# One stream of the dilated attention works in the recurrence's inverse tiles

## The chip, the core and the metric

One core of one Trainium2 chip runs the whole block. The metric is the device time of one execution in microseconds (us); lower is better. The engines are TensorE (PE in the profile, PEld its weight loads), VectorE (DVE), ScalarE (ACT), GpSimd (POOL) and SyncE (SP), which issues the DMAs in its own program order.

## What is computed

A decoder block over 1024 tokens of width 1024, in float32: a normalised and modulated input goes through one projection; mixer A is a gated delta rule with 8 heads, mixer B a dilated window attention with three groups of four heads; both are gated, projected, merged, projected again and added to the input.

```python
h = rms_norm(x, norm_w) * (1 + scale) + shift
qa, ka, va, za, beta, a, qb, kb, vb, zb, ga, gb = split(h @ w_in)
o_a = gated_delta_rule(l2(silu(conv(qa))), l2(silu(conv(ka))), silu(conv(va)), g(a), sigmoid(beta))
y_a = (rms_norm(o_a) * silu(za)) @ w_proj_a
for window, dilation in ((128, 1), (512, 4), (2048, 16)):   # 4 heads of 64 each
    o_g, lse_g = dilated_window_attention(qb, kb, vb, window, dilation)
y_b = (o_b * softmax_over_groups(lse) * silu(zb)) @ w_proj_b
x = x + gate * ((sigmoid(ga) * y_a + sigmoid(gb) * y_b) @ w_out)
out = rms_norm(x, final_norm_w)
```

In the delta rule, each chunk needs the inverse of a triangular matrix: `t_inv` is applied to the values in every step of the recurrence.

## The kernel before

The program is written by a planner. Each piece of work is a generator (a "stream") with a priority; `Sched.run` keeps an estimated clock for each engine and, whenever TensorE's estimated clock allows, steps the ready stream of the lowest priority number. So the order of every engine's instructions comes out of estimates at build time. On the chip each engine then runs its list in that order and waits by semaphores.

The main stream, `projections` (priority 99), fills TensorE with products of 512 columns: h and each weight are split into a high and a low part of reduced float32, and three products (high-high, high-low, low-high) give the accuracy. It goes over single projections first, then over seven pairs (`pair`, seven products of blocks for a two-by-two block product instead of eight), of which the last, `z8`, makes two of mixer B's gates with a silu in `block_sink`; then come the products of the merges (`tail_products`: `pa_step` for w_pa, two tiles of output interleaved at first, then w_pb) and w_out. In the profile's names pj and sb are PSUM tiles, wr and wh a weight raw and split, big a 128x1024 tile of SBUF, mid a 128x512 one.

The recurrence of mixer A runs beside the projections. `merge_stream` puts the chunk inverses of head h together in `TT[h % 2]`, one of two constant tiles of 128x8x128, and `rec_stream` reads them in its eight steps; when it is through it sets `ev_ttfree[h]`.

The attention is a list `todo_a` of 24 units: 3 groups x 2 pairs of heads x 4 pairs of blocks of 128 tokens. A worker, `attn_work`, takes the next unit, waits until the projections it reads are stored, and runs `attn_unit`: loads of q, k and v into one tile (three DMAs), scores on TensorE into two PSUM tiles, a masked maximum on VectorE into a second tile, the exponential on ScalarE there, transposes on TensorE, their copies on ScalarE, the product over the values on TensorE, a copy on VectorE, and a store to DRAM (ogd). Both tiles come from the pool `big` of 34 tiles: `big.many(2)` waits until two are free, and `big.put()` gives one back. Three workers share the list (`WORKERS = 3`, priorities 6.0 to 6.2), so up to three units are under way.

When all eight units of a group are done, `ev_og[g]` is set, and statistics of the groups are combined. `ya_split` (two streams, priority 8) reads the stored outputs of mixer A (yad), one head after the other, into two `mid` halves and splits them for the merges' products. It begins with `ev_tail`, set when the last pair begins, and takes two big tiles a head; until the last group is done it leaves `RESERVE` = 4 of them.

Of the kernel before, what the change touches and what calls it, by code (L numbers as in the profile page):

```python
# [35 lines left out]
BLOCKS = ("B11", "T2", "T1", "B21", "T3", "B22", "T4")  # L36
BLK = "x3"
BLK1 = "T1 T3 T3 T5"
WORKERS = 3
RESERVE = 4  # L40
HPRIO = 8
NW = 8
# [243 lines left out]
def hybrid_block_kernel(ctx: ExitStack, tc: tile.TileContext, x, c, norm_w, ada_w, ada_b, w_tiles, w_vb0, w_vb1,  # L286
                        w_vb2, conv_w, a_log, dt_bias, dn_norm_w, w_pa, w_pb, w_out, final_norm_w, consts, out):
    nc = tc.nc
    S = Sched(nc)
# [13 lines left out]
    big = Slots(S, bigp, "big", NBIG, [P, T])  # L303
# [7 lines left out]
    def const(shape, name, dtype=F32):  # L311
        return cp.tile(shape, dtype, name=name)
# [23 lines left out]
    TT = [const([P, 8, P], f"TT{i}") for i in range(2)]  # L336
# [901 lines left out]
    ev_ttfree = [Event() for _ in range(H)]  # L1238
# [322 lines left out]
    ev_og = [Event() for _ in range(3)]  # L1561
    pend = [0, 0, 0]

    def attn_unit(g, i2, ti):

        i0 = 2 * i2
        kf = max(i0 - 1, 0) if g == 0 else i0
        n_ = i0 + 2 - kf
        buf, sm2 = yield from big.many(2)
        qt, kt = buf[:, 0:256], buf[:, 256:256 + n_ * P]  # L1570
        v3 = buf[:, 640:640 + n_ * P].rearrange("p (a f) -> p a f", f=P)
        sp.dma_start(qt, qb_d[2 * g + ti][:, i0 * P:(i0 + 2) * P])
        sp.dma_start(kt, kb_d[2 * g + ti][:, kf * P:(i0 + 2) * P])
        if g == 0:
            src = vb_d[g].rearrange("(i p) f -> p i f", p=P)[:, kf:kf + n_]
        elif g == 1:
            src = vb_d[g].rearrange("(b p r) f -> r p b f", b=2, r=4)[i2]
        else:
            src = vb_d[g].rearrange("(p r) f -> p r f", r=8)[:, i0:i0 + 2]
        sp.dma_start(v3, src[:, :, ti * P:(ti + 1) * P])  # L1580
        yield
        tiles = []
        for i in (i0, i0 + 1):
            prev = (g == 0 and i > 0) or (g == 1 and i % 2 == 1)
            tiles.append((i, i % 2, (i - 1 if prev else i) - kf, 256 if prev else 128))
        sms = [sm2[:, sl] for sl in HALVES]
        pbs = yield from sb.many(2)
        for i, a, k0, nk in tiles:
            for hd in range(2):
                r = slice(64 * hd, 64 * hd + 64)  # L1590
                pe.matmul(pbs[hd][:, a * 256:a * 256 + nk], qt[r, a * P:(a + 1) * P], kt[r, k0 * P:k0 * P + nk], start=True,
                          stop=True)
        yield
        for hd in range(2):
            h4 = 2 * ti + hd
            sm = sms[hd]
            for i, a, k0, nk in tiles:
                msk = amask2 if g == 2 else amask if nk == 256 else amask[:, P:2 * P]
                dve.tensor_tensor_reduce(sm[:, a * 256:a * 256 + nk], pbs[hd][:, a * 256:a * 256 + nk], msk, -0.125, 3e38,
                                         op0=OP.add, op1=OP.min, accum_out=st_a[g][:, i, h4, 0:1])  # L1600
            sb.put()
            yield
            for i, a, k0, nk in tiles:
                s_ = sm[:, a * 256:a * 256 + nk]
                act.activation(s_, s_, AF.Exp, bias=st_a[g][:, i, h4, 0:1], scale=-1.0,
                               accum_out=st_a[g][:, i, h4, 1:2])
        yield
        pts = []
        for hd in range(2):
            pb = yield from sb.get()  # L1610
            n = 0
            for i, a, k0, nk in tiles:
                for b in range(nk // P):
                    pe.transpose(pb[:, n * P:(n + 1) * P], sms[hd][:, a * 256 + b * P:a * 256 + (b + 1) * P], ident)
                    n += 1
            yield
            pt = sms[hd]
            act.activation(pt[:, 0:n * P], pb[:, 0:n * P], AF.Copy)
            sb.put()
            pts.append(pt)  # L1620
        yield
        pb = yield from sb.get()
        n = 0
        for i, a, k0, nk in tiles:
            nb = nk // P
            for b in range(nb):
                for hd in range(2):
                    vv = v3[:, k0 + b, hd * 64:hd * 64 + 64]
                    pe.matmul(pb[64 * hd:64 * hd + 64, a * P:(a + 1) * P], vv, pts[hd][:, n * P:(n + 1) * P],
                              start=b == 0, stop=b == nb - 1)  # L1630
                n += 1
        yield
        big.put()
        dve.tensor_copy(pts[0][:, 0:2 * P], pb[:, 0:2 * P])
        sb.put()
        yield
        sp.dma_start(og_d[2 * g + ti][:, 2 * i2 * P:2 * (i2 + 1) * P], pts[0][:, 0:2 * P])
        big.put()
        pend[g] += 1
        if pend[g] == 8:  # L1640
            S.set(ev_og[g])

    def attn_work():
        while todo_a:
            g, ti, i = todo_a.pop(0)
            yield [ev_vbd[g], ev_qb[2 * g + ti], ev_kb[2 * g + ti], *ev_hb["T4"]]
            yield from attn_unit(g, i, ti)

    todo_a = [(g, ti, i) for g in range(3) for ti in range(2) for i in range(4)]

# [17 lines left out]
    def combine(g):  # L1668
        yield ev_sg
        scr = yield from mid.get()  # L1670
        sa = scr[:, 0:192].rearrange("p (i n) -> p i n", i=8)
        zt = scr[:, 192:288].rearrange("p (i g h) -> p i g h", i=8, g=3)
        zu = scr[:, 288:320].rearrange("p (i h) -> p i h", i=8)
        fg = fg_a[g]
        fi = fg.rearrange("p h i -> p i h")
        if g == 0:
            sp.dma_start(sa, st_d.rearrange("(i p) g n -> p i (g n)", p=P))
        elif g == 1:
            sv = st_d.rearrange("(b p r) g n -> r p b (g n)", r=4, b=2)
            s4 = sa.rearrange("p (r b) n -> p r b n", b=2)  # L1680
            for r in range(4):
                sp.dma_start(s4[:, r], sv[r])
        else:
            sp.dma_start(sa, st_d.rearrange("(p i) g n -> p i (g n)", p=P))
        yield
        s5 = sa.rearrange("p i (g h s) -> p i g h s", g=3, s=2)
        dve.tensor_tensor(zu, s5[:, :, 0, :, 0], s5[:, :, 1, :, 0], op=OP.min)
        dve.tensor_tensor(zu, zu, s5[:, :, 2, :, 0], op=OP.min)
        for q in range(3):
            dve.tensor_tensor(zt[:, :, q], zu, s5[:, :, q, :, 0], op=OP.subtract)  # L1690
        S.chain("dve", 3)
        yield
        act.activation(zt, zt, AF.Exp)
        yield
        for q in range(3):
            dst = zu if q == 0 else fi
            dve.tensor_tensor(dst, zt[:, :, q], s5[:, :, q, :, 1], op=OP.mult)
            if q:
                dve.tensor_tensor(zu, zu, fi, op=OP.add)
        dve.reciprocal(zu, zu)  # L1700
        dve.tensor_tensor(fi, zt[:, :, g], zu, op=OP.mult)
        S.chain("dve", 7)
        yield
        pb = yield from sb.get()
        pe.transpose(pb[0:32, 0:P], fg.rearrange("p h i -> p (h i)"), ident)
        yield
        act.activation(scr[0:32, 320:320 + P], pb[0:32, 0:P], AF.Copy)
        sb.put()
        yield
        sp.dma_start(fg_d[g], scr[0:32, 320:320 + P])  # L1710
        mid.put()
        yield
        S.set(ev_fg[g])
# [10 lines left out]
    ev_tail = Event()  # L1724
# [12 lines left out]
    ya_todo = list(range(8))  # L1737

    def ya_split():
        yield ev_tail  # L1740
        while ya_todo:
            h = ya_todo.pop(0)
            yield ev_ya[h]
            yield lambda: len(big.free_at) > big.debt + 1 + (0 if ev_og[2].t else RESERVE)
            hi = yield from big.get(F32R)
            lo = yield from big.get(F32R)
            ts = yield from mid.many(2)
            for q in range(2):
                sp.dma_start(ts[q], ya_d[h][:, q * 512:q * 512 + 512])
            yield  # L1750
            for q in range(2):
                act.activation(hi[:, q * 512:q * 512 + 512], ts[q], AF.Copy)
            yield
            for q in range(2):
                sl = slice(q * 512, q * 512 + 512)
                dve.tensor_tensor(lo[:, sl], ts[q], hi[:, sl].bitcast(F32), op=OP.subtract)
            mid.put(2)
            YA[h] = (hi, lo)
            S.set(ev_yas[h])
# [242 lines left out]
        S.add(attn_group(g), 7 + g * 0.01, f"attn{g}")  # L2002
    for g in range(3):
        S.add(combine(g), 7.5, f"combine{g}")
    for q in range(WORKERS):
        S.add(attn_work(), 6 + 0.1 * q, f"attnw{q}")
    S.add(ya_split(), 8, "yas")
    S.add(ya_split(), 8.1, "yas")
    S.add(yb_split(), 8, "ybs")
    S.add(yb_split(), 8, "ybs")  # L2010
# [70 lines left out]
```

## Time and profile before

| | |
|---|---|
| median of 3 runs | 1279.53 us (1276.94 to 1280.24) |
| the profiled execution | 1279.4 us, its span 1277.7 us |
| granted TensorE clock, mean | 0.995 |
| busy: PE, PEld, DVE, ACT, POOL | 98%, 81%, 60%, 39%, 14% |
| DMA | 172.03 MB, mean 135 GB/s |
| ACT table loads in 860 to 1060 us | 5, of 1283 ns |

Times within the span count from its first instruction. All instructions are issued through one helper, so every row has line L129 and is told apart by its tiles. A busy TensorE is the union of pipelined, overlapping products (a 512-wide one lasts about 0.4 us, and the next begins about 0.23 us after it); products in full float32 (scores, values) show as two. The last group of the attention falls between about 985 and 1046 us.

### The profile page before, as it was taken

What the parts mean: (1) busy time and instruction counts of PE and PEld (TensorE: products, weight loads), DVE (VectorE), ACT (ScalarE), POOL (GpSimd) and SP (SyncE); (2) the same over time, 40 slices, a digit from 0 to 9 for tenths busy, and PEclk for the clock granted to TensorE, in tenths of its full rate; (3) what the DMA queues carried; (4) which work ended last, traced back from release to release, by engine and by line L of the source; (5) the groups of instructions that cost most, each with busy time, mean ns of one, the idle gap of its engine ahead of it and who ended that gap; (6) DMA issues with size and microseconds to landing.
All of it is one profiled execution on the core that took longest, in us unless ns stands there. A gap on an engine that the chain in (4) does not pass through costs nothing.

```text
span 1277.7 us, 19213 instructions
## 1 busy us (share of the span) xinstructions
PE 1252.2 (98%) x7302; PEld 1030.8 (81%) x7302; DVE 766.9 (60%) x1528; ACT 497.9 (39%) x1079; POOL 173.9 (14%) x128
## 2 busy tenths in 40 slices
PE   7999999999999999999999999999999999999997
PEld 3689888988888978888888888887777678878886
DVE  5845893457874367864579834555555546655533
ACT  5525622346223345233462335325555852122211
POOL 4700300033001022000320002300000000002400
PEclk9999999999999999999999999999999999999999
DMA  9534433143322262341343222645455758843422
GB/s 356 200 109 148 120 92 88 67 155 114 112 75 75 73 209 65 102 115 69 107 127 103 83 76 78 225 149 156 145 137 149 251 178 255 231 162 113 143 94 83
DMA packets 112558, 172.03 MB, mean 135 GB/s; under 512 B 41009, under 2 KB 72913, under 8 KB 112466
## 3 DMA queue, kind: packets, MB, share of 16 engines
q1 hardware_dynamic: 112322, 170.55, 42.4%
q8 instruction: 57, 0.93, 0.3%
q14 instruction: 35, 0.29, 0.1%
q10 hardware_dynamic: 144, 0.26, 0.1%
HBM read 123.40 MB, written 47.37 MB: 134 GB/s over the span
## 4 chain that ended last, share of the span: by engine, by line
PE 88%; DVE 3%; DMA 3%; ACT 2%; issue 2%; POOL 1%; SPq 0%; POOLq 0%; ACTq 0%; DVEq 0%
PE pj L129 67%; PE sb L129 22%; DVE big L129 2%; ACT big L129 1%; DMA wr<-in_w_out_dram 1%; DMA big<-kbd 1%; POOL big L129 1%; DMA big<-gd 0%; ACT wh L129 0%; DVE mid L129 0%; DVE wh L129 0%; DMA wr<-in_w_pa_dram 0%; POOL wh L129 0%; ACT L129 0%; SPq L129 0%
## 5 line engine op out<-in xcount | busy, mean ns | idle before, releaser
L129 PE MATMUL pj<-big,wh 128*128 128x512 f32 x3356 | 825.2, 398 | 0.8 <-DVE big L129 0.5
L129 PEld LDWEIGHTS pj<-big,wh 128*128 128x128 f32 x3356 | 617.2, 189 | 131.9 <-issue 9.9
L129 ACT ACTIVATE wh<-wr 128x1024 fp32r<-128x1024 f32 (+3 forms) x99 | 97.5, 985 | 239.7 <-PE pj L129 223.1
L129 DVE TENSOR_TENSOR wh<-wr,wh 128x1024 fp32r<-128x1024 f32 (+3 forms) x96 | 115.2, 1200 | 64.2 <-ACT wh L129 64.0
L129 ACT ACTIVATE big<-big 128x1024 f32<-128x1024 f32 (+2 forms) x77 | 74.1, 969 | 187.2 <-DVE big L129 133.3
L129 PE MATMUL pj<-wh,big 128*128 128x256 f32 (+2 forms) x702 | 110.6, 308 | 0.5 <-POOL wh L129 0.3
L129 PE MATMUL sb<-big,wh 128*128 128x512 f32 x368 | 105.1, 423 | 0.0
L129 PEld LDWEIGHTS pj<-wh,big 128*128 128x128 f32 x702 | 96.2, 189 | 6.2 <-POOL wh L129 0.7
L129 DVE SCALAR_TENSOR_TENSOR big<-pj,cw,big 128x1023 f32<-128x1023 f32 (+2 forms) x72 | 92.1, 1279 | 1.7
L129 PEld LDWEIGHTS sb<-big,wh 128*128 128x128 f32 x368 | 66.9, 190 | 21.1 <-issue 8.4
L129 DVE TENSOR_TENSOR big<-big,big 128x1024 f32<-128x1024 f32 (+4 forms) x44 | 57.8, 1316 | 25.9 <-ACT big L129 18.8
L129 PE MATMUL sb<-sq,big 128*128 128x128 f32 x464 | 67.9, 278 | 3.0 <-ACT sq L129 2.2
L129 PEld LDWEIGHTS sb<-sq,big 128*128 128x128 f32 x464 | 63.4, 193 | 8.8 <-ACT sq L129 3.1
L129 POOL TENSOR_TENSOR wh<-wr,wh 128x1024 fp32r<-128x1024 f32 x3 | 9.1, 3036 | 348.8 <-ACT wh L129 348.8
L129 ACT ACTIVATE big<-sb 128x512 f32<-128x512 f32 (+2 forms) x80 | 40.9, 522 | 39.6 <-PE sb L129 39.5
L129 DVE SCALAR_TENSOR_TENSOR sq<-sq,gsm,sb 128x128 f32<-128x128 f32 x48 | 16.6, 345 | 63.4 <-PE sb L129 62.2
L129 DVE CUSTOM_DVE_ANT_0 big<-sb,cst 128x128 f32<-128x128 f32 (+1 forms) x96 | 29.0, 348 | 39.7 <-PE sb L129 39.7
L129 PEld LDWEIGHTS sb<-cst,big 128*128 128x128 f32 x268 | 33.9, 145 | 22.7 <-DVE rstd L129 6.8
L129 PE MATMUL sb<-cst,big 128*128 128x128 f32 x268 | 43.5, 284 | 8.0 <-DVE rstd L129 4.9
L129 PE MATMUL pj<-big,big 128*128 128x512 f32 x210 | 49.2, 390 | 0.0
L129 ACT ACTIVATE mid<-sb 128x512 f32<-128x512 f32 (+3 forms) x48 | 24.0, 500 | 60.9 <-PE sb L129 60.5
L129 DVE TENSOR_TENSOR mid<-big 64x31 f32<-64x31 f32 (+15 forms) x124 | 41.2, 332 | 8.4 <-POOL big L129 4.9
(140 smaller groups left out, 1283.5 us busy)
## 6 DMA issues: line engine op xcount, KB each, us to landing
wr<-in_w_tiles_dram SPq DMA_DIRECT2D x64, 512.0 KB, 4.2
big<-in_ada_w_dram SPq DMA_DIRECT2D x24, 512.0 KB, 9.0
big<-in_x_dram SPq DMA_DIRECT2D x16, 512.0 KB, 5.2
gd<-big SPq DMA_DIRECT2D x16, 512.0 KB, 2.9
big<-gd SPq DMA_DIRECT2D x16, 512.0 KB, 5.2
big<-grow SPq DMA_DIRECT2D x8, 512.0 KB, 5.7
vtd<-big SPq DMA_DIRECT2D x8, 512.0 KB, 2.6
big<-vtd SPq DMA_DIRECT2D x32, 128.0 KB, 4.5
```

Of the source, the lines that this page charges most:

```text
L129: r = f(*a, **k)
```

## The change

One of the three workers gets its two tiles for good: `TT[0]` for q, k and v and `TT[1]` for the scores. It starts when all eight recurrences are done (`ev_ttfree`), has priority 5.9, ahead of the other workers, and neither takes nor returns big tiles; the other two workers are as before. So the attention holds at most four big tiles at a time instead of six. `ya_split` may begin when either the last pair has begun or the last group is done.

```diff
--- before.py
+++ after.py
@@ -36,7 +36,7 @@
 BLOCKS = ("B11", "T2", "T1", "B21", "T3", "B22", "T4")
 BLK = "x3"
 BLK1 = "T1 T3 T3 T5"
-WORKERS = 3
+WORKERS = 2
 RESERVE = 4
 HPRIO = 8
 NW = 8
@@ -1561,12 +1561,12 @@
     ev_og = [Event() for _ in range(3)]
     pend = [0, 0, 0]
 
-    def attn_unit(g, i2, ti):
+    def attn_unit(g, i2, ti, own):
 
         i0 = 2 * i2
         kf = max(i0 - 1, 0) if g == 0 else i0
         n_ = i0 + 2 - kf
-        buf, sm2 = yield from big.many(2)
+        buf, sm2 = own or (yield from big.many(2))
         qt, kt = buf[:, 0:256], buf[:, 256:256 + n_ * P]
         v3 = buf[:, 640:640 + n_ * P].rearrange("p (a f) -> p a f", f=P)
         sp.dma_start(qt, qb_d[2 * g + ti][:, i0 * P:(i0 + 2) * P])
@@ -1630,21 +1630,25 @@
                               start=b == 0, stop=b == nb - 1)
                 n += 1
         yield
-        big.put()
+        if not own:
+            big.put()
         dve.tensor_copy(pts[0][:, 0:2 * P], pb[:, 0:2 * P])
         sb.put()
         yield
         sp.dma_start(og_d[2 * g + ti][:, 2 * i2 * P:2 * (i2 + 1) * P], pts[0][:, 0:2 * P])
-        big.put()
+        if not own:
+            big.put()
         pend[g] += 1
         if pend[g] == 8:
             S.set(ev_og[g])
 
-    def attn_work():
+    def attn_work(own=None):
+        if own:
+            yield ev_ttfree
         while todo_a:
             g, ti, i = todo_a.pop(0)
             yield [ev_vbd[g], ev_qb[2 * g + ti], ev_kb[2 * g + ti], *ev_hb["T4"]]
-            yield from attn_unit(g, i, ti)
+            yield from attn_unit(g, i, ti, own)
 
     todo_a = [(g, ti, i) for g in range(3) for ti in range(2) for i in range(4)]
 
@@ -1737,7 +1741,7 @@
     ya_todo = list(range(8))
 
     def ya_split():
-        yield ev_tail
+        yield lambda: ev_tail.t is not None or ev_og[2].t is not None
         while ya_todo:
             h = ya_todo.pop(0)
             yield ev_ya[h]
@@ -2002,6 +2006,7 @@
         S.add(attn_group(g), 7 + g * 0.01, f"attn{g}")
     for g in range(3):
         S.add(combine(g), 7.5, f"combine{g}")
+    S.add(attn_work([t_.rearrange("p a b -> p (a b)") for t_ in TT]), 5.9, "attnw")
     for q in range(WORKERS):
         S.add(attn_work(), 6 + 0.1 * q, f"attnw{q}")
     S.add(ya_split(), 8, "yas")
```

The order is the same up to the first unit of attention and again from the third output tile of the merges on. Between, the planner places almost every row of the attention anew. Below, big, TT, sb and pj are followed by their numbers; sta is a unit's statistics.

ScalarE, where the silus of the last pair's blocks (mid onto itself) meet the exponentials of the last group. Before:

```order
L129 ACT_TABLE_LOAD
L129 ACTIVATE mid128_8899<-mid128_8899 128x512
L129 ACTIVATE big241_8766<-sb389_8875 128x256
L129 ACTIVATE wh174_8891<-wr75_8805 128x1024
L129 ACTIVATE mid127_8869<-mid127_8869 128x512
L129 ACTIVATE wh176_8959<-wr76_8908 128x1024
L129 ACTIVATE mid122_8782<-mid122_8782 128x512
L129 ACT_TABLE_LOAD
L129 ACTIVATE big247_8856,sta2_105<-big247_8856,sta2_105 128x128 x2
```

After:

```order
L129 ACT_TABLE_LOAD
L129 ACTIVATE mid128_8939<-mid128_8939 128x512
L129 ACTIVATE mid127_8876<-mid127_8876 128x512
L129 ACT_TABLE_LOAD
L129 ACTIVATE TT1_101,sta2_105<-TT1_101,sta2_105 128x128 x2
L129 ACTIVATE big234_8923<-mid129_8944 128x512
L129 ACTIVATE big234_8923<-mid130_8945 128x512
L129 ACTIVATE wh176_8991<-wr76_8901 128x1024
L129 ACT_TABLE_LOAD
L129 ACTIVATE mid124_8809<-mid124_8809 128x512
L129 ACT_TABLE_LOAD
L129 ACTIVATE TT1_101,sta2_105<-TT1_101,sta2_105 128x128 x2
```

All three silus stood between two table loads; now the third comes later, and a set of exponentials (TT1), a merge input (big234) and the split of a weight (wh176) stand between it and the other two, with two more table loads around it.

TensorE, in the last group, beside the first merge products (pj72, pj73 before and after): transposes (cst), products over values (64x128) and products of 512. Before, the 19th and the 20th unit:

```order
L129 MATMUL sb396_9019<-cst_83,big247_8856 128x128 x2
L129 MATMUL sb397_9023<-cst_83,big247_8856 128x128 x2
L129 MATMUL pj72_8966<-big248_8880,wh172_8744 128x512 x2
L129 MATMUL pj72_8966<-big249_8881,wh172_8744 128x512 x2
L129 MATMUL pj72_8966<-big248_8880,wh173_8867 128x512 x2
L129 MATMUL sb398_9038<-big247_8856,big246_8855 64x128 x4
L129 MATMUL sb399_9043<-cst_83,big253_8942 128x128 x2
L129 MATMUL pj73_9049<-big242_8790,wh174_8891 128x512 x2
L129 MATMUL sb400_9053<-cst_83,big253_8942 128x128 x2
L129 MATMUL pj73_9049<-big243_8791,wh174_8891 128x512 x2
```

After, the 20th to the 22nd unit:

```order
L129 MATMUL sb403_9061<-cst_83,TT1_101 128x128 x2
L129 MATMUL sb404_9065<-cst_83,TT1_101 128x128 x2
L129 MATMUL sb405_9073<-cst_83,big239_8951 128x128 x2
L129 MATMUL sb406_9076<-TT1_101,TT0_100 64x128 x4
L129 MATMUL sb407_9088<-cst_83,big239_8951 128x128 x2
L129 MATMUL sb408_9113<-big239_8951,big238_8950 64x128 x4
L129 MATMUL sb409_9118<-cst_83,big241_8967 128x128 x2
L129 MATMUL pj72_8998<-big236_8927,wh172_8771 128x512 x2
L129 MATMUL sb410_9129<-cst_83,big241_8967 128x128 x2
L129 MATMUL pj72_8998<-big237_8928,wh172_8771 128x512 x2
```

Before, one unit's product stood between transposes of the next with merge products between them; now the transposes of three units and the products of two follow each other with one pair of merge products in between.

SyncE, where the own stream's 18th unit is stored and its next, the 20th, loaded; before, a place with the same kind of rows, where the 19th is stored and the 22nd loaded:

```order
L129 DMA ogd4_190<-big247_8856 128x256
L129 DMA big260_9057<-qbd5_179 128x256
L129 DMA big260_9057<-kbd5_185 128x256
L129 DMA big260_9057<-vbd2_119 128x2x128
L129 DMA mid135_9073<-yad5_125 128x512
L129 DMA mid136_9087<-yad5_125 128x512
L129 DMA ogd4_190<-big253_8942 128x256
L129 DMA big264_9102<-qbd5_179 128x256
```

After:

```order
L129 DMA wr76_8901<-in_w_pa_dram 128x1024
L129 DMA ogd4_190<-TT1_101 128x256
L129 DMA TT0_100<-qbd4_178 128x256
L129 DMA TT0_100<-kbd4_184 128x256
L129 DMA TT0_100<-vbd2_119 128x2x128
L129 DMA mid129_8944<-yad2_122 128x512
L129 DMA mid130_8945<-yad2_122 128x512
L129 DMA ogd4_190<-big227_8683 128x256
```

A unit's loads went into fresh tiles (big260); now those of one stream go into TT0, which its previous unit has read, right behind the store from TT1, and the merges' loads (yad) stand on both sides of them.

## The prediction

> **What bounds the kernel now.** I read the page first: the busy shares and the chain that ended last.
>
> ```profile
> span 1277.7 us, 19213 instructions
> PE 1252.2 (98%) x7302; PEld 1030.8 (81%) x7302; DVE 766.9 (60%) x1528; ACT 497.9 (39%) x1079; POOL 173.9 (14%) x128
> PE 88%; DVE 3%; DMA 3%; ACT 2%; issue 2%; POOL 1%; SPq 0%; POOLq 0%; ACTq 0%; DVEq 0%
> ```
>
> TensorE is the bound. Its work is the same before and after the change, so only its pauses can move the time, and what one pause costs is paid in full, because dense products stand behind it. Next I read the table of stretches of 40 us, then, where it dips, stretches of 4 us (PE, PEld, DVE, ACT, POOL busy; granted clock; DMA share).
>
> ```profile
> 960.00:1000.00 40.00, 40.00 (x243) 30.38 (x241) 18.81 (x60) 23.35 (x67) 0.00 (x0) 1.00 0.52 153
> 1000.00:1040.00 40.00, 36.44 (x227) 26.70 (x226) 22.91 (x76) 30.21 (x87) 0.00 (x0) 0.96 0.79 259
> 1040.00:1080.00 40.00, 40.00 (x190) 32.22 (x190) 21.12 (x52) 8.19 (x18) 0.00 (x0) 1.00 0.65 197
> ...
> 1012.00:1016.00 4.00, 2.88 (x18) 1.89 (x17) 2.88 (x11) 3.97 (x10) 0.00 (x0) 1.00 1.06 387
> 1024.00:1028.00 4.00, 2.71 (x18) 1.85 (x16) 1.81 (x3) 1.92 (x4) 0.00 (x0) 1.00 1.04 378
> 1028.00:1032.00 4.00, 3.27 (x13) 2.68 (x14) 2.14 (x10) 2.28 (x8) 0.00 (x0) 0.61 0.82 252
> 1032.00:1036.00 4.00, 4.00 (x25) 3.05 (x24) 1.37 (x9) 2.78 (x11) 0.00 (x0) 0.96 0.86 275
> ```
>
> The dip is the end of the attention, between the last pair of projections and the merges' products. TensorE stands for 40.00 - 36.44 = 3.56 us there, and at a clock of 0.61 and 0.96 loses another 0.39 x 4 + 0.04 x 4 = 1.7 us: 5.3 us in all, the most that a better order can win here (0.4%). The timeline of TensorE names the pauses (start, duration, what; in brackets the idle time before it):
>
> ```profile
> 1014.05 0.71 PE L129 MATMUL sb<-big 64*128 64x128 f32 x8 [0.25 <-DMA big<-kbd]
> 1016.17 0.71 PE L129 MATMUL sb<-cst,big 128*128 128x128 f32 x2 [1.04 <-ACT big L129]
> 1018.22 0.66 PE L129 MATMUL sb<-big,big 128*64 128x128 f32 x8
> 1025.18 0.60 PE L129 MATMUL sb<-cst,big 128*128 128x128 f32 x4
> 1028.73 1.13 PE L129 MATMUL sb<-big 64*128 64x128 f32 x8 [1.76 <-DMA big<-kbd]
> 1029.79 4.17 PE L129 MATMUL pj<-big,wh 128*128 128x512 f32 x12
> ```
>
> Two kinds: scores (x8 on q and k) that wait for a unit's load, and transposes that wait for ScalarE's exponentials. The first has this row in the chain, beside a quiet one; the third row gives the price of a 512-wide product, 50.18 / 220 = 0.228 us:
>
> ```profile
> 934.16 2.76 DMA big<-kbd
> ...
> 1021.69 6.90 DMA big<-kbd
> ...
> 1124.02 50.18 PE pj L129 x220
> ```
>
> A load of k lands after 2.76 us where the queues are quiet and after 6.90 us where the DMA share is near 1.
>
> **The change part by part.** I number the 24 units of attention in the order in which they are taken; 17 to 24 are the last group.
>
> *The wait of the own stream.* Its first scores stand at the same place of TensorE's order as the first scores did, so the wait for all eight recurrences costs nothing. The merges' new condition costs and brings nothing: the last group can't be done before the last pair of projections has begun, so its first half still decides. The diff has nothing else before 870 us; up to there I take the time as unchanged.
>
> *From 870 to 1000 us.* The streams now take tiles sooner, so the product over values of one unit and the scores of the same stream's next unit stand closer on TensorE. In this row of instructions a unit's follow-up costs:
>
> ```profile
> 1018.99 0.42 DVE L129 COPY big<-sb 128x256 f32<-128x256 f32 x1 [2.03 <-PE sb L129]
> 1020.78 0.38 SPq L129 DMA_DIRECT2D ogd<-big  x1
> 1021.26 0.38 SPq L129 DMA_DIRECT2D big<-qbd  x1
> 1021.69 0.85 SPq L129 DMA_DIRECT2D big<-kbd  x1
> ```
>
> Copy 0.42, store and load of q about 0.45 each on SP, then the landing of k: 0.42 + 0.9 + 2.76 + 0.2 for the handing over = 4.3 us from the end of the product, in quiet queues. The tightest places there have 15 products of 512 (3.4 us), another unit's scores (0.7) and product (0.66) and transposes between: over 5.3 us. So they are covered; I take 0 (ends 0 and +1.5).
>
> *Scores of unit 20 (own stream).* Between the product of unit 18 and these scores stand 9 products of 512 (2.05), two other units' products over values (2 x 0.66), two transposes and some 0.3 of changes: 3.9 us. Needed are 4.3 us, and 8.4 us if k takes 6.90. Also VectorE's split of a weight (1.2 us) stands ahead of the copy. Pause 0.4 to 4.5; I take 1.8, from the landing of the row at 1014.05 (k issued at 1009.44: 4.6 us). It runs beside the next item and is not added to it.
>
> *ScalarE's stretch.* The last three silus of the last pair's blocks were in one visit of the table; they are now in two, with exponentials between, so there are two more table loads, 27 for 25. The row of a load, and those of its neighbours:
>
> ```profile
> 1010.92 1.06 ACT L129 ACTIVATE wh<-wr 128x1024 fp32r<-128x1024 f32 x1 [2.34 <-PE pj L129]
> 1011.89 0.61 ACT L129 ACTIVATE mid<-mid 128x512 f32<-128x512 f32 x1
> 1012.52 1.28 ACT L129 ACT_TABLE_LOAD   x1
> 1013.82 0.40 ACT L129 ACTIVATE big<-big,sta 128x128 f32<-128x128 f32 x1
> ```
>
> and the means of the stage's groups:
>
> ```profile
> L129 ACT ACTIVATE big<-big,sta 128x128 f32<-128x128 f32 x52 | 20.4, 393 | 8.5 <-DVE sta L129 8.3
> L129 DVE TENSOR_TENSOR wh<-wr,wh 128x1024 fp32r<-128x1024 f32 x14 | 17.1, 1222 | 1.7 <-ACT wh L129 1.7
> L129 ACT ACTIVATE wh<-wr 128x1024 fp32r<-128x1024 f32 x14 | 14.8, 1056 | 20.9 <-PE pj L129 20.9
> L129 ACT ACTIVATE big<-mid 128x512 fp32r<-128x512 f32 x16 | 9.5, 626 | 4.2 <-DMA mid<-yad 4.2
> L129 ACT ACTIVATE big<-sb 128x256 f32<-128x256 f32 x16 | 5.8, 376 | 4.8 <-PE sb L129 4.8
> ```
>
> Count in the new order what ScalarE does from the split of the second merge weight (behind the copy of unit 19's second transposes) to the copy that frees unit 21's product: 2 splits (2.1), 4 table loads (5.1), 3 silus (1.9), 10 exponentials (3.9), 6 halves of the merges' inputs (3.8), 4 copies (1.5) = 18.3 us. Ahead of its first table load it waits for VectorE's split, copy and addition, 1.22 + 0.42 + 0.69 = 2.3: 20.6 us. TensorE has between the same two points 39 products of 512 (8.9), three units' scores (3 x 0.71) and products (3 x 0.66), eight transposes (1.0) and about six changes of kind at 0.2 (the first 512 after a small one): 15.2 us. ScalarE also enters the stretch some 1.2 us behind, since the four halves for the first two merges (4 x 0.63) stand ahead of the copy it begins after. So TensorE pauses 20.6 - 15.2 + 1.2 = 6.6 us in this stretch, whichever operand it waits for; the last pause, ahead of the product of unit 21, is the longest (5.5 us of ScalarE's work lie behind the last exponentials of unit 20, and only two small products and transposes on TensorE). Ends: +3.0, if ScalarE is early and the two loads (2.6) alone are uncovered; +8.5, if loads land after 6.9 us and it waits for scores too.
>
> The rule of the Trainium skill, ScalarE: Activation LUTs (What ACT_TABLE_LOAD costs), is that a switch costs a load of 1283 ns and a drain of some 1380 ns. The trace shows the 1.28 and no drain: the silu ends at 1012.50, the load starts at 1012.52, the exponential at 1013.82. By the rule two more switches would be an estimated 2.7 us dearer, and the sum 1285.7.
>
> *After it.* The scores of unit 23 again wait for the own stream's product; the last two units have 60 products of 512 beside them, where before three units had them. I take +0.5 (0 to +1.5).
>
> *The clock.* Before, a stand of 1.76 us (with 0.25 just ahead of it) was followed by 4 us at 0.61. The new pauses are longer and nearer each other; I take the same 1.7 us (0 to +3.4).
>
> The Trainium skill, TensorE: Matmul & The Clock Gate (Part 1), has the clock fall to half after an idle window of about 3.4 us. Here 1.3 us idle in the 4 us to 1028 sufficed. By the rule my pauses would hardly reach it, and the sum would lose this term: 1281.2.
>
> *Sum.* Old pauses and their clock go with the old order: -5.3. New: +6.6 (ScalarE's stretch), +0.5, +1.7 and 0 for the rest: +8.8. Net +3.5 us on the profiled execution's 1279.4 us (its span 1277.7 and 1.7 around it; the median of the runs is 1279.53, so the base serves for both): 1282.9.
>
> **The rivals.**
> *No change* (chance 0.25). The pauses move but don't grow: at the point where 96 products of 512 are left, 20 transposes and products of units remain for 24 before, one unit less to be squeezed in, and ScalarE's work ahead of its table loads could be done early. Then the new pauses are about 5.3 us as the old: 1279.4, within 2 us. Against it: ScalarE is busy 3.97 of the 4 us from 1012 already now, and gets 2.6 us more.
> *Faster* (0.10). One mechanism: loads that come early. If the own stream's loads and the scores placed ahead (units 20, 21 and 22 have theirs before any of their transposes) land in some 3 us, since the merges' loads stand one unit later in SP's queue, the exponentials are done before ScalarE's visit to the silus, and none of its extra loads lies ahead of a transpose. It decides if k lands under about 3.5 us where the DMA share is now near 1; the price is the old 5.3 less 0.5 to 1.5 left: 1275.1 at best, about 1275.5.
> *Loads, not ScalarE* (0.05). Every scores' wait of units 20 to 24 costs like the 1.76 now, the own stream's 4.5: -5.3 + 4.5 + 3 x 1.8 + 3.4 = +8.0, 1287.4.
>
> **How the numbers follow.** The forecast has the rest, 0.60. About 0.3% (3.8 us, 1275.7 to 1283.4) is what a measurement of this kernel tells from no change; the forecast's own ends are -5.3 + 3.0 = -2.3 (1277.1) and -5.3 + 8.5 + 1.5 + 3.4 = +8.1 (1287.5), most of it 1281 to 1287. Of its 0.60 I put 0.39 above 1283.4 and 0.21 within. With the rivals: slower 0.39 + 0.05 = 0.44, the same 0.21 + 0.25 = 0.46, faster 0.10. The predicted time is the forecast's, 1282.9. The range leaves the faster tenth and the highest out: 1277.8 to 1287.0.
>
> **What would show it.** Right: 27 table loads, two of them inside the stretch of the last group; a pause of 2 to 4 us on TensorE that names ScalarE, ahead of a product with 128x128 (x8), just after the own stream's; a PE share lower by 5 us or more in the 40 us that hold it; a clock under 1 behind it. The scores on TT0 waiting for a load once or twice. The same time before 1000 us within 1 us. Wrong: if TensorE's pauses in that stage sum to 4 us or less, if ScalarE shows idle time in the stretch for scores that came late (then it is the loads), or if the time differs already before 1000 us: that would be pauses at the closer scores which I set to 0.

## The result, and the profile after

The changed kernel takes 1284.88 us (median of 13 runs, 1283.16 to 1288.18) against 1279.53 us (13 runs of the kernel before beside it). The ratio is 1.0043, its 95% interval 1.0032 to 1.0054: 0.43% slower, some 5.4 us. The forecast was 1282.9. The profiled execution took 1285.0 us.

The head of its page, and the group of ScalarE's table loads (count, busy us, mean ns; then the idle time before them):

```profile
span 1283.2 us, 19212 instructions
PE 1253.4 (98%) x7302; PEld 1031.0 (80%) x7302; DVE 766.3 (60%) x1528; ACT 501.9 (39%) x1081; POOL 173.8 (14%) x128
L129 ACT ACT_TABLE_LOAD x27 | 34.6, 1283 | 26.6 <-DVE big L129 21.8
```

The end of the attention in stretches of 40 and of 4 us, as in the prediction (PE, PEld, DVE, ACT, POOL busy; granted clock; DMA share, GB/s):

```profile
1000.00:1040.00 40.00, 34.98 (x201) 25.60 (x200) 20.24 (x66) 31.51 (x86) 0.00 (x0) 0.91 0.82 267
1040.00:1080.00 40.00, 40.00 (x196) 31.80 (x195) 19.94 (x59) 10.42 (x28) 0.00 (x0) 1.00 0.52 155
...
1028.00:1032.00 4.00, 2.21 (x11) 1.64 (x12) 2.94 (x6) 2.93 (x12) 0.00 (x0) 0.71 0.96 345
1032.00:1036.00 4.00, 4.00 (x14) 2.66 (x15) 0.00 (x0) 2.53 (x6) 0.00 (x0) 0.50 0.87 276
1036.00:1040.00 4.00, 4.00 (x27) 2.94 (x26) 3.09 (x13) 1.66 (x7) 0.00 (x0) 0.94 0.46 142
```

From 1000 to 1040 us, which hold most of the last group, TensorE now stands for 5.02 us, before for 3.56. Its clock costs (0.29 + 0.50 + 0.06) x 4 = 3.4 us there, for 1.7. Between 880 and 1000 us it stands for 0.54 + 0.77 + 0.44 = 1.75 us, where it stood for 0.27 before, at a clock of 1.00 in both. The timeline of TensorE names the pauses (start, duration, what; in brackets the idle time before it and what ended it):

```profile
868.35 1.14 PE L129 MATMUL sb<-TT 64*128 64x256 f32 x8
893.44 1.13 PE L129 MATMUL sb<-TT 64*128 64x256 f32 x8 [0.54 <-DVE wh L129]
959.74 0.93 PE L129 MATMUL sb<-big 64*128 64x128 f32 x8 [0.77 <-DMA big<-kbd]
991.74 0.71 PE L129 MATMUL sb<-big 64*128 64x128 f32 x8 [0.44 <-DMA big<-kbd]
1013.47 0.71 PE L129 MATMUL sb<-TT 64*128 64x128 f32 x8 [1.85 <-DMA TT<-kbd]
1023.22 0.71 PE L129 MATMUL sb<-big 64*128 64x128 f32 x8 [0.68 <-DMA big<-kbd]
1025.81 0.44 PE L129 MATMUL sb<-cst,big 128*128 128x128 f32 x2 [0.32 <-ACT TT L129]
1026.84 0.65 PE L129 MATMUL sb<-TT,TT 128*64 128x128 f32 x6 [0.23 <-ACT TT L129]
1028.91 0.43 PE L129 MATMUL sb<-big,big 128*64 128x128 f32 x2 [1.05 <-ACT big L129]
1030.22 1.11 PE L129 MATMUL sb<-big,big 128*64 128x128 f32 x6 [0.88 <-ACT big L129]
```

These rows give a ruler that is finer than the times. The first row is the first scores of unit 1, the row at 991.74 the first scores of the last group (unit 17). The two orders are the same on TensorE up to the first, and the same again from 1048.87 on (1043.29 before). Between these ends the kernel after takes 180.5 us and the kernel before 175.7: 4.8 of the 5.6 us by which the spans differ. The rest of the program takes the same within 0.8 us. The rows of before that answer to the first scores of units 1 and 17, and its one early pause:

```profile
867.59 0.93 PE L129 MATMUL sb<-big 64*128 64x128 f32 x8
937.06 0.93 PE L129 MATMUL sb<-big 64*128 64x128 f32 x8 [0.27 <-DMA big<-kbd]
989.07 0.72 PE L129 MATMUL sb<-big 64*128 64x128 f32 x8
```

So the attention falls into two parts: up to the last group it takes 991.74 - 868.35 = 123.4 us, before 121.5 (+1.9); from there on 57.1, before 54.2 (+2.9: about half of it pauses, 5.02 for 3.56, and half the clock). The forecast put the whole loss into the second.

### The profile page after: what moved, and what is told of

Same layout as the page of the kernel before. It is cut to its first block, busy times and chain, and to the rows that moved or that the text cites. A ratio compares the mean times of both kernels' runs of the same rounds, so it can differ in the third digit from the quotient of the medians.

```text
span 1283.2 us, 19212 instructions
## 1 busy us (share of the span) xinstructions
PE 1253.4 (98%) x7302; PEld 1031.0 (80%) x7302; DVE 766.3 (60%) x1528; ACT 501.9 (39%) x1081; POOL 173.8 (14%) x128
## 5 line engine op out<-in xcount | busy, mean ns | idle before, releaser
L129 PEld LDWEIGHTS pj<-big,big 128*128 128x128 f32 x210 | 39.3, 188 | 8.4 <-POOL big L129 0.2
L129 DVE SCALAR_TENSOR_TENSOR big<-sb,s_all,big 128x128 f32<-128x128 f32 x128 | 35.2, 343 | 15.3 <-PE sb L129 15.0
L129 DVE TENSOR_TENSOR big<-big,mid 64x31 f32<-64x31 f32 (+15 forms) x124 | 41.6, 335 | 4.3
```

What stands on the lines that cost most here:

```text
L129: r = f(*a, **k)
```

## The experiments

All times are medians; a ratio is against runs of the kernel before beside it on the same chip, with its 95% interval, and need not be the quotient of the medians. The two parts are those of the ruler, each from one profile. The orders of the last four kernels meet that of before only later; their last group is 54.2 plus the difference to before where 850 of TensorE's products are left, from which point on all have the same ones to do.

| kernel | us (runs) | ratio | first part | last group |
|---|---|---|---|---|
| before | 1279.53 (13) | | 121.5 | 54.2 |
| after | 1284.88 (13) | 1.0043 (1.0032 to 1.0054) | 123.4 | 57.1 |
| after, no silus in the last pair | 1285.53 (12) | 1.0046 (1.0029 to 1.0063) | 123.6 | 55.2 |
| before, no silus in the last pair | 1277.99 (12) | 0.9994 (0.9976 to 1.0011) | 121.5 | 50.8 |
| after, no loads of the merges' inputs | 1286.64 (6) | 1.0060 (1.0038 to 1.0082) | 123.7 | 55.4 |
| after, products in the pauses | 1282.26 (12) | 1.0034 (1.0019 to 1.0049) | 123.2 | 55.4 |
| after, q and k early on SP | 1287.73 (6) | 1.0069 (1.0050 to 1.0088) | 125.5 | 58.8 |
| after, q and k early on GpSimd's queue | 1283.80 (8) | 1.0039 (1.0025 to 1.0052) | 123.0 | 56.3 |
| after, copies on GpSimd | 1283.89 (11) | 1.0041 (1.0028 to 1.0054) | 124.5 | 54.9 |
| before, copies on GpSimd | 1278.93 (12) | 1.0002 (0.9990 to 1.0014) | 121.4 | 51.4 |
| own stream in the last group only | 1280.28 (12) | 1.0002 (0.9985 to 1.0019) | 121.5 | 52.9 |
| own stream not in the last group | 1284.29 (6) | 1.0043 (1.0029 to 1.0058) | 123.4 | 56.5 |
| last group only, eased | 1277.99 (12) | 0.9999 (0.9982 to 1.0016) | 121.6 | 51.3 |
| before, eased | 1280.77 (12) | 1.0011 (0.9997 to 1.0024) | 121.4 | 54.6 |

The last column holds what the clock took in that one execution: up to two windows of 3.41 us at 0.50, each worth up to 1.7 us (last section). Differences under 2 us in it are therefore not read as gains; the ratios decide.

**Is it the table loads?** The theory of the prediction, tested with the order kept: the planner still books the silu, ScalarE gets a copy.

```diff
-                act.activation(src, src, func, scale=scale)
+                act._e.activation(src, src, AF.Copy)
+                S.book("act", "activation", src, (src, src, func), {})
```

> The changed kernel with its order kept, but the silus of the last pair of projections issued as plain copies (this leaves the silu out of two of the gates of mixer B): 21 table loads for 27, four of the six lie in ScalarE's stretch of 20 us. Theory ScalarE: the four pauses that name it (0.32 + 0.23 + 1.05 + 0.88 = 2.5 us) go, and with them part of the 3.4 us of lost clock: 1279.4 to 1282.4 us against 1284.9. Theory loads (the units' loads of k are late, whatever ScalarE does): the pauses of 1.85 and 0.68 stay, at most 0.5 us won: 1284.4 us or more.

> The control: the same edit on the kernel before, 21 table loads for 25 (the silu of the same two gates left out). Before, one pause of 1.04 us names ScalarE, the others (0.25, 1.76) a load. Theory ScalarE: 1 to 2 us faster, 1277.5 to 1278.5, so that most of the 5.4 us between the two kernels is gone when both lack these loads. Theory loads: no change within 0.5 us, and the 5.4 us stand.

The changed kernel with 21 table loads for 27 is as slow as with them (ratio 1.0046 for 1.0043), and between the two kernels without these loads the gap is as wide as ever (1.0046 and 0.9994). The theory ScalarE falls, as it was put. A row of ScalarE's timeline of this kernel, and then TensorE's, tell why:

```profile
1027.23 0.38 ACT L129 ACTIVATE TT<-sb 128x256 f32<-128x256 f32 x1 [4.56 <-PE sb L129]
```

```profile
1025.08 0.72 PE L129 MATMUL sb<-big 64*128 64x128 f32 x8
1026.76 0.60 PE L129 MATMUL sb<-cst,TT 128*128 128x128 f32 x4
1030.78 0.43 PE L129 MATMUL sb<-big,big 128*64 128x128 f32 x2 [1.05 <-ACT big L129]
1032.08 0.86 PE L129 MATMUL sb<-big,big 128*64 128x128 f32 x6 [0.88 <-ACT big L129]
```

Without its table loads ScalarE is done early and then waits 4.56 us for the transposes of unit 20, which stand on TensorE behind the scores of unit 22. The loads had filled this wait, not made one. The pauses of 1.05 and 0.88 us are the same to the hundredth: they are made by what ScalarE has to do behind those transposes.

**What stands behind them?** ScalarE's timeline of the changed kernel, with the exponentials left out:

```profile
1026.68 1.14 ACT L129 ACTIVATE big<-mid 128x512 fp32r<-128x512 f32 x2
...
1028.49 0.37 ACT L129 ACTIVATE big<-sb 128x256 f32<-128x256 f32 x1
1028.76 1.14 ACT L129 ACTIVATE big<-mid 128x512 fp32r<-128x512 f32 x2
1029.80 0.37 ACT L129 ACTIVATE big<-sb 128x256 f32<-128x256 f32 x1
```

Each of the two copies (big<-sb) that TensorE's paused products wait for has a pair of halves of the merges' inputs (big<-mid, 1.14 us) ahead of it. These were put on GpSimd, in both kernels:

```diff
-                act.activation(hi[:, q * 512:q * 512 + 512], ts[q], AF.Copy)
+                pool._e.tensor_copy(hi[:, q * 512:q * 512 + 512], ts[q])
+                S.book("act", "activation", ts[q], (ts[q], ts[q], AF.Copy), {})
```

> The changed kernel with the copies of the merges' inputs (0.57 us each on ScalarE) issued on GpSimd, which stands idle there; order of all other engines kept. Theory ScalarE's queue behind the transposes (two halves, 1.14 us, stand between the exponentials and the copy that the product of unit 21 waits for, twice): the pauses of 1.05 and 0.88 shrink to 0.5 or less, about 1.2 us and 1 to 2 us of clock behind them: stretch 177.3 to 178.5 for 180.5. Theory late loads: at most 0.5 us: 180 or more.

> The control: the same edit on the kernel before. Its one pause that names ScalarE (1.04 us) has two halves ahead of the copy: 0.5 to 1 us won, stretch 174.5 to 175.2 for 175.7. By the theory that ScalarE's halves don't matter: 175.7.

TensorE's longest pause in the last group, after with the copies on GpSimd (the next is 0.58 us, the others are under 0.3):

```profile
1014.98 1.23 PE L129 MATMUL sb<-TT 64*128 64x128 f32 x8 [2.96 <-DMA TT<-kbd]
```

The two pauses are gone, so their cause is shown; but the wait for TT's load in the same place as the 1.85 is now 2.96, with a clock of 0.85 and 0.73 in the two stretches of 4 us from 1012; and the pause ahead of unit 17, 0.44 before the copies moved, is 1.35 (first part 124.5). The last group shrinks by 2.2 us in the profile, but the ratio is 1.0041 (1.0028 to 1.0054) for 1.0043: no gain that the runs can tell. In the kernel before it changes nothing that the runs can tell either (1.0002).

**Is it the loads?** First, the 4.2 MB of the merges' inputs were taken off the queues (they read a constant tile instead):

```diff
-                sp.dma_start(ts[q], ya_d[h][:, q * 512:q * 512 + 512])
+                S.book("dma", "dma_start", ts[q], (ts[q],), {})
...
-                act.activation(hi[:, q * 512:q * 512 + 512], ts[q], AF.Copy)
+                act.activation(hi[:, q * 512:q * 512 + 512], cst[:, 0:512], AF.Copy)
```

> The changed kernel, TensorE's order kept, with the loads of the merges' inputs left out (the merges read a constant tile instead of mixer A's output): 16 loads of 256 KB, 4.2 MB, less on the queues beside the last group. ScalarE does the same work, but waits for no such load. Theory loads: the pauses of 1.85, 0.68 and 0.44 us that name loads go, and part of the clock's loss: 1279 to 1282.4 us. Theory ScalarE: its table loads stay, at most 1 us won: 1284 us or more.

```profile
1000.00:1040.00 40.00, 35.20 (x208) 26.20 (x208) 20.50 (x66) 33.20 (x90) 0.00 (x0) 0.96 0.57 176
...
1015.34 0.71 PE L129 MATMUL sb<-TT 64*128 64x128 f32 x8 [2.18 <-DMA TT<-kbd]
```

The DMA share from 1000 to 1040 falls from 0.82 to 0.57, and the pause ahead of unit 20's scores is still 2.18 us; the time is no better (1.0060). So the load isn't late because the merges' loads share the queues. Whether other loads slow it was not tested: the DMA share is still 0.92 in the 4 us from 1011. The next two kernels issue it earlier, q and k of the own stream's next unit right behind the scores of its present one, from SP's queue and from GpSimd's (`pool._e`):

```diff
+        sp._e.dma_start(buf[:, 0:256], qb_d[2 * g + ti][:, i0 * P:(i0 + 2) * P])
+        sp._e.dma_start(buf[:, 256:256 + (i0 + 2 - kf) * P], kb_d[2 * g + ti][:, kf * P:(i0 + 2) * P])
...
+        if own:
+            own_next(buf, g, ti, i2)
```

> The changed kernel, every other engine's order kept, with q and k of the own stream's next unit issued right behind the scores of its present one (six of its units; its q and k are not read after the scores) instead of behind the copy and the store of its result. The stretch of the attention on TensorE, from the first row where the two orders part to the first where they are the same again, is 180.5 us after and 175.7 before. Theory late loads (k is issued too late, whatever else is on the queues): the pauses that name TT's load go (1.85 in the last group, 0.3 to 0.7 ahead of it), 2 to 2.5 us and up to 1 us of clock: stretch 177 to 178.6. Theory ScalarE's queue: the pause moves from the scores to the transposes behind them, under 0.7 us won: 179.8 or more.

> As the run with early q and k, but these twelve loads are issued from GpSimd's queue, so that SP's queue isn't held behind the own stream's scores. Theory SP's queue (in that run the other streams' loads came late because SP waited for those scores): its pauses of 1.94 and 1.09 on the big tiles' loads go, those of TT's loads too: stretch 177.5 to 179, 1281.5 to 1283.5. Theory that early loads only move the pause to VectorE and ScalarE: the pauses of 1.35 and 1.86 us that name them stay: 180.5 or more, 1284.5 or more.

The pause ahead of unit 20's scores is gone in both. From GpSimd's queue the time is 1.0039 for 1.0043, no gain that the runs can tell, with these pauses of TensorE:

```profile
959.60 0.93 PE L129 MATMUL sb<-big 64*128 64x128 f32 x8 [1.47 <-DMA big<-kbd]
1013.68 3.47 PE L129 MATMUL pj<-big,wh 128*128 128x512 f32 x14 [1.35 <-DVE mid L129]
1028.68 0.43 PE L129 MATMUL sb<-big,big 128*64 128x128 f32 x2 [1.06 <-ACT big L129]
```

The scores start in time, and the next product waits for VectorE instead (1.35); ScalarE's pause of 1.05 stands as it was. The time, and the two parts together (179.2 us), lie between the two expectations, so neither is borne out: the pause of 1.09 us on another stream's load is gone, the one of 1.94 is still 1.47. From SP's queue the early loads make it worse (1287.73; first part 125.5, of which 1.7 us is the clock, at 0.50 from 960.4 to 963.8). SP's rows, and the row of TensorE that waits:

```profile
953.02 0.62 SPq L1576 DMA_DIRECT2D TT<-qbd  x1
953.68 0.53 SPq L1577 DMA_DIRECT2D TT<-kbd  x1
955.23 0.44 SPq L129 DMA_DIRECT2D big<-kbd  x1
...
959.18 0.93 PE L129 MATMUL sb<-big 64*128 64x128 f32 x8 [1.94 <-DMA big<-kbd]
```

The two issues take 1.3 us ahead of another stream's loads, and the pause ahead of its scores grows from 0.77 to 1.94 us. Counted from the scores of unit 12, k is issued 0.7 us later than in the changed kernel, and it lands after 3.82 us for 3.35: that is the growth. From GpSimd's queue it is issued no later, but lands after 4.31, beside the early loads (pause 1.47). So SP's list is a part of it, the slower landing the rest.

**The clock.** Products that nobody reads were put in the pauses at 1013.47, 1028.91 and 1030.22, with no wait made shorter (the first eight ahead of unit 20's scores, the others ahead of unit 21's first products over values):

```diff
+        if (g, ti, i2) == (2, 0, 3):
+            for _ in range(8):
+                pe._e.matmul(pbs[0][:, 128:256], ident, cst[:, 0:128], start=True, stop=True)
...
+                    if (g, ti, i2, a) == (2, 1, 0, 0):
+                        for _ in range(2):
+                            pe._e.matmul(pb[:, 256:512], ident, cst[:, 0:256], start=True, stop=True)
```

> The changed kernel with products that nobody reads in two pauses of TensorE: eight of 128 columns ahead of the scores of unit 20 (pause 1.85 us), two of 256 columns ahead of each of the first two products over values of unit 21 (pauses 1.05 and 0.88 us). No wait is shorter. Theory clock (the idle time lowers the clock in the 8 us behind it, worth 3.4 us): the slow stretches go, 2 to 3.4 us won, 1281.5 to 1283 us. If the low clock isn't due to these pauses: the same to 0.5 us slower, 1284.9 to 1285.4.

```profile
1000.00:1040.00 40.00, 37.67 (x232) 28.25 (x231) 20.91 (x66) 32.63 (x91) 0.00 (x0) 1.00 0.87 276
```

The clock stays at 1.00 where it was 0.91, and the last group is 1.7 us shorter in the profile. The ratio is 1.0034 for 1.0043, with overlapping intervals: that these pauses lower the clock is seen in the profile, what it is worth in the time isn't settled.

**In which group?** The own stream in the last group alone (a third stream in the big tiles until then), and the counterpart, the own stream in groups 0 and 1 alone:

```diff
+            yield lambda: not todo_a or todo_a[0][0] == 2
...
+            if early and todo_a[0][0] == 2:
+                return
```

```diff
+            if own and todo_a[0][0] >= 2:
+                return
+            if late and todo_a[0][0] < 2:
+                yield lambda: not todo_a or todo_a[0][0] >= 2
+                continue
```

> The own stream takes units of the last group alone; groups 0 and 1 are done by three streams in the big tiles as before, and the third of these ends there. 25 table loads. If the two orders cost what the pauses of their places say (1.5 us in groups 0 and 1, the rest in the last group): stretch 179.0, time 1283. If the loss of the last group comes only from the state in which the streams enter it: as before, 175.7 and 1279.

> The counterpart of the run with the own stream in the last group alone: the own stream takes units of groups 0 and 1 and ends there, a third stream in the big tiles takes its place in the last group. 27 table loads. If the loss comes from the closer scores in groups 0 and 1 and from the state in which they leave the streams: as the whole change, 1283 to 1285.5, stretch 179 to 181. If it comes from the own stream's units in the last group: the 1.5 us of idle time ahead of 1000 us stay and the rest goes, stretch 177.2, 1280.5 to 1281.5.

These two runs decide the place. With the own stream in the last group alone the time is that of before (1.0002); with it in groups 0 and 1 alone it is that of the whole change (1.0043, the same figure). And the first part of the ruler is 121.4 to 121.6 us in all six kernels whose groups 0 and 1 are done in big tiles, and 123.0 to 125.5 in all eight with the own stream there, whatever else was edited. TensorE's rows of the counterpart show the same three early pauses as the whole change; its last group, without TT, still takes 56.5 us:

```profile
893.23 1.13 PE L129 MATMUL sb<-TT 64*128 64x256 f32 x8 [0.52 <-DVE wh L129]
959.51 0.93 PE L129 MATMUL sb<-big 64*128 64x128 f32 x8 [0.76 <-DMA big<-kbd]
991.64 0.71 PE L129 MATMUL sb<-big 64*128 64x128 f32 x8 [0.55 <-DMA big<-kbd]
```

**Can both be beaten?** The own stream in the last group alone, and the kernel before, each with the copies on GpSimd and the last pair's silu done where its gate is read:

```diff
-            sink = block_sink(z_d[j], ev_zd[j], AF.Silu)
+            sink = block_sink(z_d[j], ev_zd[j])
...
+            if j < 2:
+                act.activation(z, z, AF.Silu)
+                yield
             r = (1, 4, 8)[g]
```

> A version meant to beat both: the own stream in the last group alone, the copies of the merges' inputs on GpSimd, and the silu of the last pair done when its gate is read for mixer B (not where it is produced, so that no table load stands between exponentials). The two pauses that name ScalarE there (1.02 and 0.50) go, the load's 0.77 stays: 1 to 2.5 us less than that kernel's 1280.3: 1277.5 to 1279.5. If what is won turns into waits for loads: 1279.5 to 1281.

> The kernel before with the same two easings (copies of the merges' inputs on GpSimd, the late silu). Each alone (the silus without their table loads; the copies on GpSimd) left the time as it was, while the profiled stretch was 172.3 and 172.9 us for 175.7. If the easings add up: 1275.5 to 1278, stretch 171.5 to 173. If the loads end last anyway: 1278 to 1280.

Neither is told from the kernel before (0.9999 and 1.0011). The first profiles at 51.3 us in the last group, 2.9 us less than before (1.7 of them because its clock stays at 1.00 in that execution), but over twelve runs nothing of it is left that the measurement can see. In the second, TensorE's longest pause and the 4 us behind it are these:

```profile
1027.56 0.78 PE L129 MATMUL sb<-big 64*128 64x128 f32 x8 [3.21 <-DMA big<-kbd]
...
1028.00:1032.00 4.00, 4.00 (x16) 3.04 (x13) 3.69 (x11) 1.65 (x8) 3.13 (x4) 0.57 0.91 287
```

With ScalarE eased, a load is waited for at the place of before's 1.76.

## Why the prediction was right or wrong

The time and its sign came out (1284.9 within 1277.8 to 1287.0, 2.0 us above the forecast), the main cause did not; that the total agrees is luck, as the terms show.

*The old pauses, -5.3.* They went with the old order, as said. The merges' new condition does nothing, as said: built without it the changed kernel is the same program, instruction for instruction, and so is the kernel before built with it.

*870 to 1000 us, taken as 0 (0 to +1.5).* This is the step that failed. It measured 1.75 us of idle time for 0.27, at its upper end, and 1.9 us in the first part, above it. It rested on "4.3 us from the end of the product" to the next scores of a stream, the unit's own copy, store and loads. The longest of the three early pauses stands ahead of the scores at 959.74, unit 13. The stream's last unit before it is the 11th. Its product, its copy (the second of the row of two), its store and the load of k are in these rows (TensorE, VectorE, SP, and the load's row of the chain):

```profile
949.30 0.88 PE L129 MATMUL sb<-big,big 128*64 128x128 f32 x12
950.93 1.22 DVE L129 TENSOR_TENSOR wh<-wr,wh 128x1024 fp32r<-128x1024 f32 x1
952.66 0.75 DVE L129 COPY big<-sb 128x256 f32<-128x256 f32 x2
951.13 3.79 SPq L129 DMA_DIRECT2D qbd<-mid  x2
955.01 0.62 SPq L129 DMA_DIRECT2D ogd<-big  x1
956.26 3.35 DMA big<-kbd
```

The product ends at 950.18; its copy begins at 953.00, 2.8 us later, since VectorE has a weight's split, an addition and another unit's copy (the first of the two) ahead of it in its list; the store leaves SP at 955.01, behind two stores of the projections that wait for VectorE too; k is issued at 956.26 and lands after 3.35: 9.4 us for 4.3. The instructions of the unit were priced right, what stands ahead of them in two queues was left out.

The other two early pauses have the same ahead of their loads on SP, two stores of the projections in a row:

```profile
884.75 4.07 SPq L129 DMA_DIRECT2D qbd<-mid  x2
983.99 3.74 SPq L129 DMA_DIRECT2D kbd<-mid  x2
```

Such a pair holds SP for some 4 us, where one store takes 0.5. Between 880 and 1000 us the changed kernel has four pairs, of which three end in a pause, and the kernel before has one. Nearness alone, on which the step was judged, is not what costs: up to unit 17, the nearest follow-ups of the changed kernel stand 5.7 to 7.5 us behind their stream's product (8.0 at least before), and none of them waits, as 4.3 us foretold; the three that wait stand 9.5, 9.6 and 14.3 us behind. That the pairs make these pauses is read from the timelines; no run took them apart.

The Trainium skill, TensorE: Matmul & The Clock Gate (Architectural detail, on queue depths), says that ScalarE and VectorE take their instructions strictly first in, first out. The rows agree: the copy waited 2.8 us behind instructions that it doesn't depend on.

*Scores of unit 20, 1.8 beside the next item.* The size was right (1.85), the place wrong: ScalarE stood idle meanwhile, so this pause is on the path:

```profile
1013.78 1.28 ACT L129 ACT_TABLE_LOAD   x1 [2.40 <-issue]
```

*ScalarE's stretch, +6.6.* The 40 us hold 5.0 us of pauses, but only 0.32 + 0.23 + 1.05 + 0.88 = 2.5 name ScalarE, none of them is the 2 to 4 us that the prediction gave as its sign (the longest is 1.05), and they are as long without the table loads. The step set all of ScalarE's work in the stretch (20.6 us) against all of TensorE's (15.2); but the two meet in the middle, at the transposes of unit 20. Ahead of them ScalarE has 4.56 us to spare without the four table loads of 5.1; behind them it is late with or without.

*Behind it, +0.5:* 0 (40.00 of 40 us busy from 1040). *The clock, +1.7:* 3.4, two windows of 3.41 us at 0.50 where before had one; how many there are depends in part on chance (last section). The sum by measured sizes is -5.3 + 1.5 + 5.0 + 3.4 = +4.6, the ruler's 4.8: two terms too large and two too small met near the right total, by luck.

*The rivals.* "Loads, not ScalarE" (0.05) was nearer to the cause than the forecast in the last group, where loads end 2.5 of the 5.0 us, and the only one to name them; but no rival put the loss ahead of the last group. The mark set out for it, "if the time differs already before 1000 us", is the one that showed. (The best of the rival "Faster" is mis-added: 1279.4 - 5.3 + 0.5 is 1274.6, not 1275.1. Nothing hangs on it.)

What stays open is why the last group itself takes longer (54.9 to 58.8 us, against 50.8 to 54.6) when the own stream has worked in groups 0 and 1. Without half of TensorE's busy time at a clock of 0.50, it is 53.3 to 55.7 against 50.8 to 52.9: the clock's chance isn't the reason. It was shown that it does, also with that stream gone; which detail of the order handed over makes it was not.

## What to carry to other kernels

An extra buffer that lets a stream start earlier places its steps anew among everyone else's; price the way from one to the next by what already stands in the in-order queues between the two (VectorE's list, SP's list), not by the stream's own instructions alone, nor by how near the two stand. Where two engines hand work to and fro, balance them between one meeting point and the next, not over a stage: work that fits into a wait is free, and the same work behind the meeting point is paid in full. And when a total agrees with a forecast, run the experiment that divides it by place before believing the cause.

## What the runs showed of the hardware

*The granted clock is 1.00 or 0.50, and changes only at fixed points.* In all 14 profiles the points at which it changes lie whole multiples of 3.413 us apart over the whole execution; in the changed kernel it is 0.50 from 1029.66 to 1036.49 us, two such windows, before from 1028.87 to 1032.28, one. A value such as 0.71 is the mean of a stretch cut across such a point. Cut at the points (columns as above), first the changed kernel, then the kernel before:

```profile
1009.18:1012.59 3.41, 2.43 (x24) 1.65 (x22) 3.41 (x6) 2.19 (x4) 0.00 (x0) 1.00 0.86 259
1012.59:1016.01 3.42, 2.54 (x16) 2.15 (x17) 2.65 (x12) 2.22 (x3) 0.00 (x0) 1.00 0.98 291
...
1026.25:1029.66 3.41, 1.81 (x12) 0.91 (x12) 1.87 (x4) 3.41 (x12) 0.00 (x0) 1.00 1.02 405
1029.66:1033.07 3.41, 2.85 (x13) 2.22 (x14) 1.47 (x3) 1.66 (x7) 0.00 (x0) 0.50 0.86 276
```

```profile
1025.46:1028.87 3.41, 1.39 (x13) 0.86 (x13) 1.14 (x3) 0.78 (x3) 0.00 (x0) 1.00 0.91 317
```

*What decides is TensorE's idle time within one window, not the longest pause.* The changed kernel's longest pause, 1.85 us, falls across a point, leaves 0.98 and 0.88 us idle in two windows and costs no clock. Pauses of 1.05 us and less put 1.60 us into the window to 1029.66, and 0.50 follows. The kernel before has 2.02 us in the window to 1028.87, where the prediction read 1.3 us in the 4 us to 1028. From 60 to 1265 us, over the 14 profiles, every window at 1.00 with 1.7 us idle or more was followed by 0.50 and, with one exception, none with less than 1.4; between the two both occur. A window at 0.50 with 0.4 us idle or more was followed by another (here 0.56 us), and one with less by 1.00, with the same exception (the run without silus, 6.8 us at 0.50 from 394 us with no idle time in the window ahead of it). Where the points fall differs from execution to execution, so the same pauses can cost 0, 1.7 or 3.4 us.

The Trainium skill, TensorE: Matmul & The Clock Gate (Part 1), speaks of an idle window of about 3.4 us ahead of half clock; the length agrees with the 3.413 us here, but the window need not be idle throughout: 1.60 us of it were enough.
